# First projection of a two-layer attention kernel in a written order: half of its channels transposed first, its six norms by two powers, epsilon as a column of the squares

## The chip, the cores and the metric

The kernel runs as one program on one core of a Trainium2 chip. The metric is the device time of an execution in microseconds, lower is better. The engines are TensorE (PE; its weight loads are PEld), VectorE (DVE), ScalarE (ACT), GpSimd (POOL) and SyncE (SP, which issues most of the DMAs). Each engine works off its own queue in the order in which the built program lists its instructions, and waits on semaphores of the others.

## The reference, cut to what matters

Two layers over 512 latent tokens and 256 context tokens, model width 1024. What the change touches is the first step of layer 0:

```python
mod_x = silu(c) @ w_ada + b_ada            # shift, scale, gate for latent tokens
mod_c = silu(c_ctx) @ w_ada + b_ada        # the same for context tokens
hx = rmsnorm(x, norm_g) * (1 + scale_x) + shift_x
hc = rmsnorm(ctx, norm_g) * (1 + scale_c) + shift_c
px = hx @ w_in                             # a_k, a_v, b_k, b_v, a_q, b_q, a_z, b_z, g_a, g_b
ka = rmsnorm(a_k per head of 64, k_norm_a) # likewise qa, qb, kb
```

`rmsnorm` divides by sqrt(mean(x*x) + 1e-6). Neighbourhood attention, grouped-query attention, gated merging, an output projection and a residual follow, in both layers; layer 1 computes only the latent stream at its end.

## The kernel before, in words

All products are in fp32 split in a high and a low part (`hi`, `lo`), three TensorE passes of 128x512 each: `hi*whi`, `hi*wlo`, `lo*whi` (lines 352 to 356, `mm3`). The low part is made by a subtraction on DVE or GpSimd (`load_w`, line 316; for weights, 327; for activations, 314).

**The opening of layer 0** builds the normalised, modulated input with channels on partitions. There are six token tiles of 128 (four latent, two context) and eight channel tiles k of 128.

- `load_x` (128) issues the six loads of x on SP, mixed with the small inputs, the first weights of the modulation and the first weight tile of the projection.
- silu of the conditioning vectors is made of a tanh (143) and two DVE operations (145, 146), transposed (151) and copied to `scol`; the small parameters are transposed to `gcol`.
- `start_y` (289), once per token tile: ACT squares the tile and sums (294), GpSimd adds epsilon (261) and raises to -0.5 (263, both in `rstd`, 258), DVE scales the tile (296), TensorE transposes its eight channel blocks in two halves of four (300), DVE copies the first half and ACT the second out of PSUM into `yT` (302).
- The modulation's shift and scale come in five parts, `PARTS` (35): channel tiles 0; 1 and 2; 3 and 4; 5 and 6; 7. A part is `ada_load` (177, one 1 MB load per channel tile), `ada_part` (190: matmuls of four 32-column groups, then a copy of the row on ACT, 199) and `ada_turn` (202: transposes, a reduce, and three small DVE operations in `mod_finish`, 168).
- `start_mod` (304) applies scale and shift to a channel tile in place (311, DVE), casts its high part (313, ACT) and subtracts for the low part (314, DVE, and GpSimd for k = 2 and 5). The first two channel tiles (`START`, 36) go in three pieces of 256 tokens, the others whole.
- The first projection (a_k, lines 594 to 610) holds all six token tiles in six PSUM banks and adds the channel tiles part by part. After the third and the fourth token tile (`AT`, 34) the next part's matmuls and its transposes are put on TensorE.

What orders this: the framework's scheduler, from a simulated timeline, sets the order of each engine's instructions; `behind` (388) pins single groups on one engine behind what was recorded before them.

**After it** the six a_k tiles are copied out of PSUM, squared, reduced and normalised one by one (`evac_na`, 447; `head_rstd`, 409; `mul_heads`, 416), and turned to channels by `turn` (424) some tiles later. `head_rstd` makes a square of 512 columns on ACT (411), a reduce per head on DVE (413) and, through `rstd`, an add and a power on GpSimd. It serves a_k, a_q, b_k and b_q in both layers: 44 calls, 32 of them with 8 heads, 12 with 2. The same `rstd` serves six token tiles in front of layer 1 (`make_hx`, 266). The next projection, a_v, follows at once (line 629): its weights go through three `raw` buffers and are split on ACT, DVE and GpSimd.

Of the kernel before, what the change touches and what calls it, by code (L numbers as in the profile page):

```python
# [14 lines left out]
DM = 1024  # L15
# [17 lines left out]
ON_PE, ON_DVE = mybir.EngineType.PE, mybir.EngineType.DVE  # L33
AT = (2, 3)
PARTS = ((0, 1), (1, 3), (3, 5), (5, 7), (7, 8))
START = 2
# [15 lines left out]
def hybrid_kernel(es: ExitStack, tc, x, ctx, cvec, w_ada, w_ada0, small, gvec, w_in, w_o_a, w_o_b, w_out,  # L52
# [72 lines left out]
    xts0 = []  # L125
    npool = es_n.enter_context(tc.tile_pool(name="nrm", bufs=2, reuse_waits="tile"))

    def load_x(t):
        xt = npool.tile([128, DM], F32, tag="x", name=nm("x"), bufs=XB)
        nc.sync.dma_start(xt, x_src(t))  # L130
        xts0.append(xt)

    load_x(0)
    S.dma_start(ident, ident_d)
    S.dma_start(stg, small)
    nc.sync.dma_start(crow, cvec)
    load_x(1)
    ehalf = cp.tile([128, 8], F32, name="ehalf")
    G.memset(ehalf, -0.5)


    cth = stp.tile([16, 128], F32, name="cth")
    S.activation(cth, crow, AF.Tanh, scale=0.5)
    csl = stp.tile([16, 128], F32, name="csl")
    V.scalar_tensor_tensor(csl, cth, 1.0, crow, ALU.add, ALU.mult)
    V.tensor_scalar(csl, csl, 0.5, None, ALU.mult)
    asum = cp.tile([128, 24, 2, 2], F32, name="asum")
    scol = stp.tile([128, 8, 32], F32, name="scol")
    V.memset(scol, 0.0)
    pt = psw(16, "t")  # L150
    T.transpose(pt, csl, ident[0:16, 0:16])
    V.tensor_copy(scol[:, :, 0:2], pt.rearrange("p (v k) -> p k v", v=2))
    gcol = cp.tile([128, 68], F32, name="gcol")
    pt = psw(68, "t")
    T.transpose(pt, stg, ident[0:68, 0:68])
    V.tensor_copy(gcol, pt)
    bsc = cp.tile([128, 2, 8], F32, name="bsc")
    V.tensor_scalar(bsc, gcol[:, 0:32].rearrange("p (l a k) -> p l a k", l=2, a=2)[:, :, 1, :], 1.0, None, ALU.add)
    g32 = cp.tile([128, 2, 8], F32, name="g32")
    V.tensor_scalar(g32, gcol[:, 32:48].rearrange("p (l k) -> p l k", l=2), 32.0, None, ALU.mult)  # L160
# [3 lines left out]

    def raw_tile():
        return wp.tile([128, 512], F32, tag="raw", name=nm("raw"), bufs=3)
# [10 lines left out]
    def ada_load(q, pool):  # L177

        ws, (k0, k1) = [], PARTS[q]
        for k in range(k0, k1):  # L180
            w = (pool.tile([128, 2048], F32, tag="rawx", name=nm("rawx"), bufs=RX) if k % 2 == 0
                 else big("rawy")[:, 0:2048])
            nc.sync.dma_start(w, w_ada0[k])
            w = w.rearrange("p (i n) -> p i n", n=256 * (k1 - k0))
            ws += [w[:, i, :] for i in range(w.shape[1])]
        return ws

    ada_row = []

    def ada_part(q, ws, pool):  # L190

        k0, k1 = PARTS[q]
        m = k1 - k0
        pt = psw(256 * m, "t")
        for i, w in enumerate(ws):
            j = i % 4
            T.matmul(pt[32 * j:32 * j + 32], scol[:, i, :], w, start=i < 4, stop=i > 3)
        row = pool.tile([128, 512], F32, tag="row", name=nm("row"), bufs=1)
        S.copy(row[:, :256 * m], pt)
        return row  # L200

    def ada_turn(q, row, pool):

        k0, k1 = PARTS[q]
        m = k1 - k0
        pt = psw(256 * m, "t")
        for f in range(2 * m):
            T.transpose(pt[:, 128 * f:128 * f + 128], row[:, 128 * f:128 * f + 128], ident)
        sums = pool.tile([128, 2, 2, 2], F32, tag="sums", name=nm("sums"))
        V.tensor_reduce(sums.rearrange("p a f v -> p (a f) v") if m == 2 else sums[:, :, 0],  # L210
                        pt.rearrange("p (f j v) -> p f v j", f=2 * m, j=4)[:, :, 0:2, :], AX, ALU.add)
        mod_finish(0, sums[:, :, 0:m], k0, k1)
# [45 lines left out]
    def rstd(ss, n, eps_n, w):  # L258

        a = sp.tile([128, 8], F32, tag="rsa", name=nm("rsa"))  # L260
        G.tensor_scalar(a[:, :w], ss, eps_n, None, ALU.add)
        b = sp.tile([128, 8], F32, tag="rsb", name=nm("rsb"))
        G.tensor_tensor(b[:, :w], a[:, :w], ehalf[:, :w], ALU.pow)
        return b[:, :w]

    def make_hx(l, t, xt, hx, pool):
# [4 lines left out]
        rs = rstd(ss, 1, DM * EPS, 1)  # L271
        y = pool.tile([128, DM], F32, tag="y", name=nm("y"), bufs=1)
        V.tensor_scalar(y, xt, rs, None, ALU.mult)
# [15 lines left out]
    def start_y(t, pool, yT):  # L289

        xt = xts0[t]
        junk = pool.tile([128, DM], F32, tag="junk", name=nm("junk"), bufs=1)
        ss = sp.tile([128, 1], F32, tag="ss1", name=nm("ss1"))
        S.activation(junk, xt, AF.Square, accum_out=ss)
        rs = rstd(ss, 1, DM * EPS, 1)
        V.tensor_scalar(xt, xt, rs, None, ALU.mult)
        for h in range(2):
            pt = psw(512, "t")
            for k in range(4):
                T.transpose(pt[:, 128 * k:128 * k + 128], xt[:, 512 * h + 128 * k:512 * h + 128 * k + 128], ident)  # L300
            d = yT[h].rearrange("p (k n) -> p k n", k=4)[:, :, 128 * t:128 * t + 128]
            (S.copy if h else V.tensor_copy)(d, pt.rearrange("p (k n) -> p k n", k=4))

    def start_mod(k, yT, hx, cuts):

        d = yT[k // 4].rearrange("p (k n) -> p k n", k=4)[:, k % 4, :]
        hi, lo = hx_k(hx, 0, k), hx_k(hx, 1, k)
# [180 lines left out]
    def layer(l, hx, nxt, mid):  # L488
# [105 lines left out]
        if first:  # L594
            w, pss = [], [psw() for t in range(6)]
            for q, (k0, k1) in enumerate(PARTS):
                mid(q, lambda: w.extend(load_w(W, C_AK, 512, k1 - k0, mix_lo, k0)))
                for k in range(k0, k1):
                    start_mods(k)
# [569 lines left out]
```

## Time and profile before

| | us |
|---|---|
| median of 3 runs | 1156.32 |
| range of the runs | 1155.41 to 1157.58 |
| the profiled execution's own time | 1156.21 |
| its span, first to last instruction | 1154.4 |
| TensorE busy | 1125.2 (97%) |
| VectorE busy | 811.8 (70%) |
| ScalarE busy | 574.2 (50%) |
| GpSimd busy | 496.5 (43%) |

Durations come from the profiled execution. Matmuls are pipelined: the time of one in the timeline contains its latency, and the distance between two starts is its slot. A row of the timeline is: start, time, engine, line, operation, output and inputs, shape, count, and in brackets how long the engine was idle before and what ended it. A row of the groups is: line, engine, operation, tiles, count, then busy time, mean ns of one, then the idle time before them and its releaser.

### The profile page before, as it was taken

How to read it: one execution, taken by the hardware profiler on the slowest of the kernel's cores; microseconds unless marked ns; L12 is line 12 of the kernel's file. 1: busy time of each engine (PE TensorE's matmuls, PEld its weight loads, DVE VectorE, ACT ScalarE, POOL GpSimd, SP SyncE). 2: the span in 40 equal slices, each digit the busy share in tenths (PEclk: the TensorE clock that was granted, in tenths of full speed). 3: DMA queues.
4: the chain of work that ended last, by engine and by line, in shares of the span. 5: the costliest groups of instructions: out<-in, count | busy, mean ns of one | idle time of the engine just before them, and what ended most of it. 6: DMA issues, size and time to landing. Idle time of an engine off the chain costs nothing.

```text
span 1154.4 us, 17322 instructions
## 1 busy us (share of the span) xinstructions
PE 1125.2 (97%) x6094; PEld 947.6 (82%) x6094; DVE 811.8 (70%) x1512; ACT 574.2 (50%) x1168; POOL 496.5 (43%) x459
## 2 busy tenths in 40 slices
PE   6999999999999999999999999999999999999998
PEld 4688888989988888878788787888888988887786
DVE  5566588997464687698488755569787665798563
ACT  5353266666333465566330265346666445766521
POOL 2362354454265243354411127245563664365321
PEclk9999999999999999999999999999999999999999
DMA  9534222233332332370343423543332333142233
GB/s 380 186 122 138 71 83 65 83 113 97 107 128 65 105 101 73 72 271 19 131 161 103 171 74 110 179 106 113 104 105 82 110 101 102 64 173 92 64 127 93
DMA packets 87999, 134.04 MB, mean 116 GB/s; under 512 B 10628, under 2 KB 52584, under 8 KB 86248
## 3 DMA queue, kind: packets, MB, share of 16 engines
q1 hardware_dynamic: 87696, 132.83, 35.6%
q8 instruction: 48, 0.79, 0.3%
q14 instruction: 39, 0.32, 0.1%
q10 hardware_dynamic: 216, 0.10, 0.0%
HBM read 115.58 MB, written 17.32 MB: 115 GB/s over the span
## 4 chain that ended last, share of the span: by engine, by line
PE 80%; DVE 9%; issue 4%; ACT 3%; POOL 2%; DMA 2%; SPq 0%; POOLq 0%; ACTq 0%; DVEq 0%
PE psx L356 11%; PE psx L354 11%; PE psx L355 11%; PE psf L354 9%; PE psf L356 9%; PE psf L355 9%; PE pst L676 4%; PE pss L725 2%; PE pss L726 2%; PE psv L980 2%; PE pss L802 1%; PE psv L979 1%; PE pst L429 1%; DVE ptl L680 1%; DVE wlo L341 1%
## 5 line engine op out<-in xcount | busy, mean ns | idle before, releaser
L680 DVE TENSOR_TENSOR ptl<-pst,pth 128x512 fp32r<-128x512 f32 (+1 forms) x176 | 116.0, 671 | 46.6 <-ACT pth L679 45.6
L679 ACT CAST pth<-pst 128x512 fp32r<-128x512 f32 (+1 forms) x176 | 99.3, 576 | 87.1 <-PE pst L676 56.1
L341 POOL TENSOR_TENSOR wlo<-raw,whi 128x512 fp32r<-128x512 f32 x68 | 95.6, 1411 | 104.8 <-ACT whi L339 84.1
L354 PE MATMUL psf<-hx,whi 128*128 128x512 f32 (+1 forms) x368 | 139.2, 378 | 1.0 <-ACT zt L514 1.0
L355 PE MATMUL psf<-hx,whi 128*128 128x512 f32 (+1 forms) x368 | 138.2, 375 | 0.0
L356 PE MATMUL psf<-hx,wlo 128*128 128x512 f32 (+1 forms) x368 | 137.9, 375 | 0.0
L354 PE MATMUL psx<-whi,hx 128*128 128x512 f32 (+1 forms) x368 | 137.8, 376 | 0.0
L355 PE MATMUL psx<-wlo,hx 128*128 128x512 f32 (+1 forms) x368 | 135.6, 368 | 0.0
L356 PE MATMUL psx<-whi,hx 128*128 128x512 f32 (+1 forms) x368 | 134.9, 369 | 0.0
L327 POOL TENSOR_TENSOR wlo<-raw,whi 128x512 fp32r<-128x512 f32 x44 | 63.6, 1447 | 137.6 <-ACT whi L324 121.0
L339 ACT CAST whi<-raw 128x512 fp32r<-128x512 f32 x136 | 82.5, 621 | 55.0 <-DMA raw<-in_w_in_dram 36.5
L324 ACT CAST whi<-raw 128x512 fp32r<-128x512 f32 x96 | 58.6, 622 | 101.2 <-PE psx L356 39.9
L676 PE MATMUL pst<-ident,p 128*128 128x128 f32 x640 | 99.9, 272 | 1.4 <-DVE ptl L680 0.8
L341 DVE TENSOR_TENSOR wlo<-raw,whi 128x512 fp32r<-128x512 f32 x68 | 71.5, 1053 | 29.7 <-ACT whi L339 29.0
L676 PEld LDWEIGHTS pst<-ident,p 128*128 128x128 f32 x640 | 77.8, 140 | 13.0 <-DVE ptl L680 1.3
L665 POOL TENSOR_SCALAR r<-r 128x1 f32<-128x1 f32 x64 | 22.5, 351 | 152.5 <-DVE r L660 145.5
L666 POOL TENSOR_TENSOR p<-p,r 128x512 f32<-128x512 f32 (+1 forms) x64 | 84.2, 1315 | 5.1 <-POOL r L665 0.2
L354 PEld LDWEIGHTS psx<-whi,hx 128*128 128x128 f32 x368 | 69.5, 189 | 13.5 <-issue 2.9
L356 PEld LDWEIGHTS psf<-hx,wlo 128*128 128x128 f32 x368 | 69.4, 189 | 11.8
L354 PEld LDWEIGHTS psf<-hx,whi 128*128 128x128 f32 x368 | 69.4, 189 | 11.8 <-ACT zt L514 1.2
L356 PEld LDWEIGHTS psx<-whi,hx 128*128 128x128 f32 x368 | 69.4, 189 | 11.7
L355 PEld LDWEIGHTS psx<-wlo,hx 128*128 128x128 f32 x368 | 69.6, 189 | 10.6
(239 smaller groups left out, 3033.8 us busy)
## 6 DMA issues: line engine op xcount, KB each, us to landing
raw<-in_w_in_dram SPq DMA_DIRECT2D x168, 256.0 KB, 2.9
rawb<-in_w_ada_dram SPq DMA_DIRECT2D x64, 256.0 KB, 2.7
gs<-zt SPq DMA_DIRECT2D x32, 256.0 KB, 2.0
raw<-in_w_out_dram SPq DMA_DIRECT2D x32, 256.0 KB, 2.9
tg<-gs SPq DMA_DIRECT2D x4, 1536.0 KB, 6.7
rawx<-in_w_ada_dram SPq DMA_DIRECT2D x4, 1024.0 KB, 9.1
rawy<-in_w_ada_dram SPq DMA_DIRECT2D x4, 1024.0 KB, 8.9
raw<-in_w_o_a_dram SPq DMA_DIRECT2D x16, 256.0 KB, 2.8
```

What stands on the lines that cost most here:

```text
L324: S.copy(hi[:, :n], raw[:, :n])
L327: e.tensor_tensor(lo[:, :n], raw[:, :n], F(hi[:, :n]), ALU.subtract)
L339: S.copy(hi, raw)
L341: lo_eng(i).tensor_tensor(lo, raw, F(hi), ALU.subtract)
L354: T.matmul(ps, lhs[0], rhs[0], start=first, stop=False)
L355: T.matmul(ps, lhs[0], rhs[1], start=False, stop=False)
L356: T.matmul(ps, lhs[1], rhs[0], start=False, stop=last)
L666: G.tensor_tensor(p[:, c0:c1], p[:, c0:c1], r[:, i:i + 1].to_broadcast([128, c1 - c0]), ALU.mult)
L676: T.transpose(pt[:, c0:c0 + 128], src, ident)
L679: S.copy(hi[:, n0:n1], pt[:, n0:n1])
L680: V.tensor_tensor(lo[:, n0:n1], pt[:, n0:n1], F(hi[:, n0:n1]), ALU.subtract)
L725: T.matmul(ps[:, c0:c0 + n], q, sl(kh), start=True, stop=False)
```

## The change

It does three things.

1. **The opening and the first projection are written out by hand** (`start`), and `in_turn` pins the written order on TensorE, DVE, ACT and GpSimd. `wake` puts matmuls of a zero tile on TensorE at three places (six, one and three of 128x256). Only the first four channel blocks of each token tile are transposed ahead of the first products (`start_turn(t, 0)`); the second halves (`start_turn(t, 1)`) follow during k = 0, 1 and 2. The modulation goes in the parts 0; 1; 2 and 3; 4 and 5; 6 and 7, and every channel tile in three pieces of 256 tokens. All low parts of this stage are on DVE. The products run channel tile by channel tile.
2. **Epsilon rides along.** The token tiles get a 1025th column that holds sqrt(1024 * 1e-6), the heads' squares a 65th that holds 64 * 1e-6, so that the sum contains it, and the add on GpSimd goes, except in `make_hx`.
3. **The six norms of a_k** are summed in two groups of three tiles (24 columns each), with one power for each group.

The core of the diff:

```diff
-PARTS = ((0, 1), (1, 3), (3, 5), (5, 7), (7, 8))
-START = 2
+PARTS = ((0, 1), (1, 2), (2, 4), (4, 6), (6, 8))
+TURN = (1, 3)
+AKG, YB = ((0, 1, 2), (3, 4, 5)), 5
+WT = (0, 1)
...
     def load_x(t):
-        xt = npool.tile([128, DM], F32, tag="x", name=nm("x"), bufs=XB)
-        nc.sync.dma_start(xt, x_src(t))
-        xts0.append(xt)
+        xe = npool.tile([128, DM + 1], F32, tag="x", name=nm("x"), bufs=XB)
+        G.memset(xe[:, DM:DM + 1], (DM * EPS) ** 0.5)
+        xe0.append(xe)
+        xts0.append(xe[:, 0:DM])
+        nc.sync.dma_start(xts0[t], x_src(t))
...
+    ada_load(0)
+    load_raw(0)
+    for t in range(2, 6):
+        load_x(t)
+    for k in (1, 2):
+        ada_load(k)
+        load_raw(k)
+    ada_load(3)
...
+    V.memset(zero, 0.0)
+    S.activation(cth, zero[0:16, 0:128], AF.Tanh)
...
+    def wake(n, cols):
+        pt = psw(512, "t")
+        for i in range(n):
+            T.matmul(pt[:, :cols], zero[:, 0:128], zero[:, :cols], start=True, stop=True)
...
+    def start_ss(t):
+        junk = npool.tile([128, DM + 1], F32, tag="junk", name=nm("junk"), bufs=1)
+        ss = sp.tile([128, 1], F32, tag="ss1", name=nm("ss1"))
+        S.activation(junk, xe0[t], AF.Square, accum_out=ss)
+
+        def rest():
+            G.tensor_tensor(ss, ss, ehalf[:, 0:1], ALU.pow)
+            V.tensor_scalar(xts0[t], xts0[t], ss, None, ALU.mult)
+        return rest
...
+    def head_ss(ps, nh, ss):
+        sq = hp["sq"][0]
+        hp["sq"].reverse()
+        S.activation(sq[:, :nh, 0:HD], ps.rearrange("p (h d) -> p h d", d=HD), AF.Square)
+        V.tensor_reduce(ss, sq[:, :nh], AX, ALU.add)
+
+    def head_pow(ss, n):
+        G.tensor_tensor(ss, ss, ehalf[:, :n], ALU.pow)
...
+            def evac_ak(ts):
+                n = 8 * len(ts)
+                ss = sp.tile([128, 32], F32, tag="ss32", name=nm("ss32"), bufs=1)
+                for i, t in enumerate(ts):
+                    y = hp["p"].tile([128, 512], F32, tag="y", name=nm("y"), bufs=YB)
+                    (V.tensor_copy if t % 2 else S.copy)(y, pss[t])
+                    head_ss(y, 8, ss[:, 8 * i:8 * i + 8])
+                    ys.append(y)
+                head_pow(ss[:, :n], n)
+                for i, t in enumerate(ts):
+                    mul_heads(ys[t], ys[t], ss[:, 8 * i:8 * i + 8], 8)
+                    to_channels(ys[t], 4, kav, t, False, gk)
...
+    def in_turn(fn):
+        for e in (ON_PE, ON_DVE, ON_ACT, ON_POOL):
+            fn = lambda e=e, fn=fn: behind(e, fn)
+        fn()
...
+        def body():
+            wake(6, 256)
+            norm0 = start_ss(0)
+            tanh()
+            norm0()
+            silu()
+            norm1 = start_ss(1)
+            silu_b()
+            constants()
+            out0 = start_turn(0, 0)
+            wake(1, 256)
+            row0 = ada_part(0)
+            out0(S.copy)
+            norm1()
+            out1 = start_turn(1, 0)
+            hi0 = split_hi(raw0[0])
+            w.append(split_lo(raw0[0], hi0, V))
+            row0()
+            mod0 = ada_turn(0)
+            wake(3, 256)
+            out1(V.tensor_copy)
+            norm2 = start_ss(2)
+            mod0()
+            lo = start_mod(0, 0, 256)
+            norm3 = start_ss(3)
+            norm2()
+            prod(0, 0, 0)
+            prod(0, 1, 0)
+            lo(V)
...
+            for k in range(1, KT):
+                q = next(i for i, (k0, k1) in enumerate(PARTS) if k0 <= k < k1)
+                more = k == PARTS[q][0] and q + 1 < len(PARTS)
+                pieces = [(256 * i, 256 * i + 256) for i in range(3)]
+                for t in range(6):
+                    prod(k, t)
+                    if more and t == TURN[0]:
+                        row = ada_part(q + 1)
+                        row()
+                    if more and t == TURN[1]:
+                        ada_turn(q + 1)()
+                    if k + 1 < KT:
+                        d = t - (3 if k == 1 else 0)
+                        if 0 <= d < 3:
+                            los.append(start_mod(k + 1, *pieces.pop(0)))
+                            if d > 0:
+                                los.pop(0)(V)
+                        if d == 2:
+                            los.pop(0)(V)
+                        if t == WT[0]:
+                            hi = split_hi(raw0[k + 1])
+                        if t == WT[1]:
+                            w.append(split_lo(raw0[k + 1], hi, V))
+                    if later and t % (4 - k) == 0:
+                        start_turn(later.pop(0), 1)(S.copy)
+                    if t == 4 and k + 3 < KT:
+                        load_raw(k + 3)
+                        if k + 4 < KT:
+                            ada_load(k + 4)
...
```

In the built program SP issues, after the first nine loads, the modulation weights and weight tiles as their buffers come free; the two broadcast loads of `cd` (the silu vectors) and the first two tiles of layer 1's modulation (`rawb`) stand ahead of the second weight tile of a_v, where before they stood behind all eight. Beside this stage the instructions of the rest of the program are the same but for the norms' adds and tiles, in an order that the scheduler has changed at some places.

288 lines of the change are left out of this document (162 added, 126 removed).

## The prediction

> **What bounds the kernel now.** I read the page first, then the windows (columns: length, TensorE, its weight loads, VectorE, ScalarE, GpSimd, granted clock, DMA share, GB/s), the waits and the timeline of the first 70 us.
>
> ```profile
> PE 1125.2 (97%) x6094; PEld 947.6 (82%) x6094; DVE 811.8 (70%) x1512; ACT 574.2 (50%) x1168; POOL 496.5 (43%) x459
> ```
> ```profile
> 0.00:10.00 10.00, 2.56 (x10) 1.93 (x10) 3.44 (x12) 4.05 (x7) 1.93 (x9) 1.00 0.84 297
> 10.00:20.00 10.00, 8.08 (x54) 5.68 (x55) 6.34 (x16) 8.20 (x17) 4.56 (x9) 1.00 1.02 420
> 60.00:70.00 10.00, 10.00 (x46) 8.17 (x45) 7.26 (x12) 7.90 (x15) 5.77 (x6) 1.00 0.34 103
> ```
> ```profile
> PE pst L151 <- DVE csl L146: 6.6, 1, 6.6
> PE pst L429 <- ACT sq L411: 0.7, 1, 0.7
> ```
>
> TensorE is busy for 97% of the span and idle for 29.2 us; 9.4 of these lie in the first 20 us (the second and the first window: 10 - 2.56 and 10 - 8.08). From 60 us on its windows are full. So time can be won in the opening, until the first product and through the first projection, and a microsecond won there goes through to the end. The head norms hardly hold TensorE: one wait of 0.7 us is charged to a chain with a norm in it.
>
> The timeline gives the stage's marks.
>
> ```profile
> 7.72 1.97 PE L300 MATMUL pst<-ident,x 128*128 128x128 f32 x8 [0.51 <-DVE scol L152]
> ...
> 11.97 1.94 PE L197 MATMUL pst<-rawx,scol 128*32 128x256 f32 x16
> ...
> 14.68 1.09 PE L300 MATMUL pst<-ident,x 128*128 128x128 f32 x8
> ...
> 18.20 1.09 PE L300 MATMUL pst<-ident,x 128*128 128x128 f32 x8 [0.68 <-DVE yT L302]
> ...
> 19.05 0.47 PE L354 MATMUL psf<-whi,hx 128*128 128x512 f32 x1
> ...
> 20.53 0.60 PE L300 MATMUL pst<-ident,x 128*128 128x128 f32 x4
> ...
> 20.89 0.48 PE L354 MATMUL psx<-whi,hx 128*128 128x512 f32 x1
> ...
> 27.42 0.50 PE L354 MATMUL psf<-whi,hx 128*128 128x512 f32 x1 [0.31 <-ACT hx L313]
> ```
> ```profile
> 32.10 1.07 PE L197 MATMUL pst<-rawy,scol 128*32 128x512 f32 x8
> ...
> 33.96 0.50 PE L354 MATMUL psx<-whi,hx 128*128 128x512 f32 x1
> ...
> 55.58 1.07 PE L197 MATMUL pst<-rawy,scol 128*32 128x256 f32 x16
> 56.58 0.50 PE L354 MATMUL psx<-whi,hx 128*128 128x512 f32 x1
> ...
> 65.16 0.39 PE L354 MATMUL psf<-whi,hx 128*128 128x512 f32 x1
> ```
> ```profile
> 19.53 0.23 PE psf L355
> ```
>
> The first product starts at 19.05, the second channel tile (k = 1) at 27.42, the next projection at 65.16. A product's slot is 0.23 us (the chain). A modulation part of two tiles takes 1.86 (32.10 to 33.96), of one tile 1.00 (55.58 to 56.58) where TensorE is quick, and four transposes 0.36 (20.53 to 20.89). TensorE also has a slow state: eight transposes took 1.97 at 7.72 and 1.09 at 14.68, one tile's part 1.94 at 11.97 and 1.00 later, though the granted clock stands at 1.00 in all these windows. So between 27.42 and 65.16 there are 37.7 us, of which 126 products are 29.0, three parts 1.86 + 1.86 + 1.00 = 4.7, three small turns at most 1.1: some 2.9 us were waits.
>
> **The change part by part.** The sum is against the profiled run's own 1156.21 us (span 1154.4 and 1.8 around it), 0.1 below the median of 1156.32. The terms are these rows (the groups of 0 to 64 us with shapes apart; then loads).
>
> ```profile
> L296 DVE TENSOR_SCALAR x<-x,rsb 128x1024 f32<-128x1024 f32 x6 | 4.5, 752 | 2.2 <-POOL rsb L263 2.2
> L302 DVE COPY yT<-pst 128x512 f32<-128x512 f32 x6 | 4.1, 685 | 1.6 <-PE pst L300 1.6
> L302 ACT COPY yT<-pst 128x512 f32<-128x512 f32 x6 | 3.5, 586 | 5.3 <-PE pst L300 5.2
> L263 POOL TENSOR_TENSOR rsb<-rsa,ehalf 128x1 f32<-128x1 f32 x6 | 3.5, 575 | 0.5
> L314 DVE TENSOR_TENSOR hx<-yT,hx 128x256 fp32r<-128x256 f32 x6 | 2.4, 422 | 0.7 <-ACT hx L313 0.7
> L313 ACT CAST hx<-yT 128x256 fp32r<-128x256 f32 x6 | 2.3, 408 | 2.0 <-DVE yT L311 2.0
> L311 DVE TENSOR_SCALAR yT<-yT,modc 128x256 f32<-128x256 f32 x12 | 4.7, 409 | 0.1
> L199 ACT COPY row<-pst 128x256 f32<-128x256 f32 x2 | 0.7, 372 | 5.4 <-PE pst L197 5.4
> L324 ACT CAST whi<-raw 128x512 fp32r<-128x512 f32 x15 | 8.8, 619 | 1.4 <-DMA raw<-in_w_in_dram 1.4
> ```
> ```profile
> 6.50 1.16 ACT junk L294 x2
> ```
> ```profile
> 23.51 0.69 DVE L327 TENSOR_TENSOR wlo<-raw,whi 128x512 fp32r<-128x512 f32 x1
> ...
> 25.83 0.18 DVE L210 TENSOR_REDUCE sums<-pst 128x8 f32<-128x32 f32 x1
> ...
> 26.52 1.84 DVE L311 TENSOR_SCALAR yT<-yT,modc 128x256 f32<-128x256 f32 x5
> ```
> ```profile
> 2.10 0.43 SPq L183 DMA_DIRECT2D rawx<-in_w_ada_dram  x1
> ...
> 5.31 1.11 SPq L130 DMA_DIRECT2D x<-in_ctx_dram  x2
> ```
> ```profile
> DMA to landing us min/median/max: 6.9/9.1/12.7
> ```
> ```profile
> x<-in_ctx_dram SPq DMA_DIRECT2D x1, 512.0 KB, 8.7
> ```
>
> *Opening.* The first nine loads keep their order on SP, so the first modulation weights land at 9.0 (2.10 + 6.9) and the last token tile near 14.7 (the second of the pair, issued near 6.0, + 8.7). All else that the first part needs (x0 scaled, silu turned) is small work that I put done by 8.7. The part therefore starts at 9.1 instead of 11.97, because x1's and half of x0's transposes no longer stand ahead of it, and takes 1.0 instead of 1.94 if the six zero matmuls, issued from about 1.2 us, have made TensorE quick: done at 10.1. Row copy 0.37 and two transposes: 10.9. DVE must first do x1's scaling, a weight's low part and x1's copy (0.69) and is free at 11.6; reduce and three small operations are 0.69 (25.83 to 26.52): 12.3. Scale-and-shift 0.41, cast 0.41, some 0.05 a hand-off: **first product at 13.3**, 5.8 earlier. The zero matmuls themselves lie where TensorE waits; only the single one ahead of the first part can cost, at most 0.2.
>
> *Rest of k = 0.* On ACT the squares of x3, x4, x5 now stand behind that cast: 3 x 1.16 from 13.2 to 16.7 (x5 is there in time), then x3's copy to 17.3; DVE, after x4's scaling, ends the second piece's scale-and-shift at 17.8; cast 18.2: third and fourth token tile. TensorE's six products end at 19.7, x5's transposes 20.1, second part 21.1; ACT copies x5 (20.2 to 20.8), splits a weight 0.62, and after DVE's scale-and-shift casts the third piece at 22.0; k = 0 ends at 23.5. The second part's sums reach DVE at 22.9; 0.69 + 0.41 + 0.41 with hand-offs: **k = 1 starts at 24.5**, 2.9 ahead of now. Of 5.8 half is given back: TensorE waits about 3 us of these 11 for ACT and DVE.
>
> *k = 1 to 7.* More work has been put off than now: five second-half transposes 5 x 0.36 = 1.8, and the parts left are 3 x 1.86 = 5.6. With 29.0 of products and three turns 1.1 this is 37.5 us: 62.0 without any wait. Waits that the order leaves: 0.2 for a PSUM bank in k = 1, and 0.1 where k = 2 begins (its chain from the turn is 0.69 + 0.41 + 0.41 and hand-offs, 1.75, against 0.36 + 6 x 0.23 of cover). From then on each piece is made a channel tile ahead: DVE has 3 x 0.41 + 3 x 0.42 + 0.7 (a weight's low part, 23.51) = 3.2 us a tile against 4.1 of products, now that GpSimd makes no low parts here. I take 0.3 of waits, between 0 and the 2.9 of now: next projection at 62.3 instead of 65.16, **-2.9**.
>
> *The order of loads.* From k = 1 on each weight tile waits on SP for the split three tiles before, with a modulation load behind it. The fifth of these (for k = 2's part at 33.7) is issued near 22.7, the seventh near 35 for 45; the longest landing above, 12.7, would cost 1.7 and 2.7, the median nothing. I take nothing.
>
> *Norms.*
>
> ```profile
> L263 POOL TENSOR_TENSOR rsb<-rsa,ehalf x56: 569/1666/2149, 6.2 to 934.9; 128x8 f32<-128x8 f32 x32, 128x1 f32<-128x1 f32 x12, 128x2 f32<-128x2 f32 x12
> L261 POOL TENSOR_SCALAR rsa<-ss x56: 218/244/743, 5.9 to 934.6; 128x8 f32<-128x8 f32 x32, 128x1 f32<-128x1 f32 x12, 128x2 f32<-128x2 f32 x12
> ```
>
> 50 of the 56 adds go (the six in front of layer 1 stay): 50 x 0.24 = 12 us of GpSimd, which is busy 43%. Six powers of 8 columns, 6 x 1.67 = 10.0, become two of 24. No row shows 24 columns: from 0.575 for one and 1.67 for eight, 0.16 a column, I estimate 4.2 each; three times the longest row, 6.4, is the other end, three times 0.57 the low one. The first can begin when the third square is summed, near 67, and its tile's transposes stand some 56 slots behind the new projection's start, near 75: 67 + 4.2 + 0.7 = 72 or, at 6.4, 74. Hidden. Reduces over 65 columns instead of 64, eight small memsets and 1025 columns in a square are under 2% of their rows, beside TensorE. Waits of TensorE on norms: 0.7 and little else; I take **-0.4**, between 0 and -1.0.
>
> Sum: 1156.21 - 2.9 - 0.4 = 1152.9; on the median's footing **1153.0 us**.
>
> [...] The rows show that 16 transposes from 7.72 did not make TensorE quick and that it was quick at 14.68, 2.7 us after ordinary matmuls began at 11.97. [...]
>
> **The rivals.**
> - *TensorE is slow where I count it quick* (zeros do not warm it, or it falls back between the products of k = 0). For: 7.72. Against: 18.20. Price: the part +0.94 and x0's and x1's half transposes +0.4 each ahead of the first product, or about 2.7 us of doubled work after 18.3, so 1.4 to 2.7: 1155.2.
> - *The fixed order keeps the waits*: four engines each in one written order, so that every piece waits for the last of DVE and ACT; 2.9 of waits stay, or k = 1 starts nearer 27. 1156.0. For: half the lead is lost in k = 0 already. Against: 3.2 of DVE against 4.1.
> - *Slower: the next projection's weights come late.* They go through three buffers, and SP now issues the two broadcast loads and two modulation tiles ahead of the second of them. The fourth waits for GpSimd's low part of the first, near 56.8, and is needed at 64.3 after 1.3 of splitting; 6.0 us of landing decide.
>
> ```profile
> DMA to landing us min/median/max: 2.5/3.4/11.3
> ```
>  At the longest, 11.3, TensorE would stand 5.3: 1158.3. Against: the DMA share is 0.34 at 60 us, and 3.4 is the middle.
> - *That it does not do what it says* is out: the built program's instructions stand in the new order on all four engines, and the rest differs little.
>
> **How the numbers follow.** Forecast 0.58 (1151.5 to 1154.6), slow TensorE 0.15, waits kept 0.17, late weights 0.10. A measurement of this kernel tells about 0.2%, 2.3 us, from no change: faster means below 1154.0. Of the forecast 0.5 lies below, 0.08 above; of the two middle rivals 0.02 below, 0.28 within, 0.02 above; late weights are 0.02 within (a small delay) and 0.08 above. Faster 0.52, same 0.38, slower 0.10. The range leaves a tenth on each side: 1150.8 (no waits, norms -1.0, a walk 0.9 shorter) to 1157.4 (the lower late-weights cases).
>
> **What would show it.** First product at 13.3 and not past 14.5; the first part at 1.0 us; k = 1 at 24.5; the next projection at 62.3, after gaps that sum to 0.3; two powers of about 4 us with no wait at the transposes near 75; the rest at its present length. It is wrong if TensorE's 128-column transposes still take 0.25 us after 8 us, if k = 1 begins after 26, or if the new projection waits for whi or wlo.

## The result, and the profile of the changed kernel

The changed kernel took 1151.69 us (median of 8 runs, 1150.48 to 1154.22) where the kernel before took 1155.47 (8 runs, 1153.94 to 1157.58): ratio 0.9969, 95% interval 0.9959 to 0.9978, so 3.8 us less. A second comparison of the same two kernels (11 runs and 33) gave 0.9977, 0.9968 to 0.9986, 2.7 us less. The forecast was 1153.0. The sum came out near; two of its terms did not, and one of the rivals takes part in most executions, as far as their mean granted clock tells.

The profiled run of the changed kernel took 1150.48 us (span 1148.7), the fastest of its eight, and that of before 1156.21, slower than its median. The two profiles therefore stand 5.7 us apart where the medians stand 2.7 to 3.8: one profile must not be read as the kernel here.

Totals of the changed kernel's page, then its first windows (columns: length, TensorE, its weight loads, VectorE, ScalarE, GpSimd, granted clock, DMA share, GB/s):

```profile
PE 1127.1 (98%) x6114; PEld 951.2 (83%) x6114; DVE 811.4 (71%) x1541; ACT 578.8 (50%) x1185; POOL 467.1 (41%) x405
```
```profile
0.00:10.00 10.00, 7.44 (x28) 5.12 (x32) 3.13 (x12) 4.94 (x9) 1.63 (x13) 1.00 0.83 294
10.00:20.00 10.00, 8.09 (x51) 5.40 (x43) 6.80 (x15) 7.00 (x14) 2.37 (x4) 1.00 1.02 414
```

TensorE's idle time in the first 10 us fell from 7.4 to 2.6, most of it filled with zeros; what the opening gained has to be read from marks. The timeline of TensorE, in the places that the prediction named:

```profile
1.17 5.49 PE L187 MATMUL pst<-zero 128*128 128x256 f32 x12 [1.17 <-DVE zero L179]
...
9.58 1.07 PE L231 MATMUL pst<-rawx,scol 128*32 128x256 f32 x16
...
13.53 0.50 PE L1141 MATMUL psf<-whi,hx 128*128 128x512 f32 x1
...
24.60 0.53 PE L1141 MATMUL psf<-whi,hx 128*128 128x512 f32 x1 [0.25 <-ACT hx L350]
...
25.44 0.60 PE L338 MATMUL pst<-ident,x 128*128 128x128 f32 x4
25.79 0.48 PE L1141 MATMUL psx<-whi,hx 128*128 128x512 f32 x1
26.11 0.39 PE L1142 MATMUL psx<-wlo,hx 128*128 128x512 f32 x1
...
63.35 0.39 PE L401 MATMUL psf<-whi,hx 128*128 128x512 f32 x1
```

First product 13.53 (forecast 13.3), second channel tile 24.60 (24.5), next projection 63.35 (62.3; 65.16 before). So in this execution the opening is worth 1.8 us and not 2.9. The rows from 25.44 show one reason: four transposes take 0.35 until the product behind them starts, and that product takes 0.32 where the others take 0.23. The other 3.9 us of the two spans' difference lie behind the first projection, and need another account.

The waits of TensorE hold the first hint of it. The row of before in which a norm held TensorE (0.7 us, near 704) has no successor; the largest rows that are left are those of before, the one of L199 apart, which was 6.6 there (L151):

```profile
PE psv L1042 <- DVE ptl L742: 2.0, 3, 1.5
PE pst L736 <- DVE ptl L742: 1.5, 3, 0.8
PE pst L199 <- DVE csl L195: 1.3, 1, 1.3
PE psx L401 <- DVE ho L751: 1.2, 1, 1.2
```

### The profile page after: what moved, and what is told of

Its sections match the earlier page's. It is cut to its first block, busy times and chain, and to the rows that moved or that the text cites. A ratio compares the mean times of both kernels' runs of the same rounds, so it can differ in the third digit from the quotient of the medians.

```text
span 1148.7 us, 17395 instructions
## 1 busy us (share of the span) xinstructions
PE 1127.1 (98%) x6114; PEld 951.2 (83%) x6114; DVE 811.4 (71%) x1541; ACT 578.8 (50%) x1185; POOL 467.1 (41%) x405
## 4 chain that ended last, share of the span: by engine, by line
PE 84%; DVE 6%; ACT 3%; DMA 2%; issue 2%; POOL 1%; SPq 0%; ACTq 0%; POOLq 0%; DVEq 0%
PE psx L403 12%; PE psx L402 12%; PE psx L401 12%; PE psf L401 9%; PE psf L402 9%; PE psf L403 9%; PE pst L738 5%; PE pss L787 2%; PE pss L788 2%; PE pss L864 2%; PE psv L1042 2%; PE pst L487 1%; PE psv L1041 1%; DMA rawb<-in_w_ada_dram 1%; DVE ptl L742 1%
## 5 line engine op out<-in xcount | busy, mean ns | idle before, releaser
L388 POOL TENSOR_TENSOR wlo<-raw,whi 128x512 fp32r<-128x512 f32 x68 | 96.3, 1419 | 99.1 <-ACT whi L386 76.2
L374 POOL TENSOR_TENSOR wlo<-raw,whi 128x512 fp32r<-128x512 f32 x40 | 55.2, 1381 | 163.1 <-ACT whi L371 155.3
L401 PE MATMUL psx<-whi,hx 128*128 128x512 f32 (+1 forms) x328 | 121.3, 371 | 0.0
L402 PE MATMUL psx<-wlo,hx 128*128 128x512 f32 (+1 forms) x328 | 119.9, 366 | 0.0
L403 PE MATMUL psx<-whi,hx 128*128 128x512 f32 (+1 forms) x328 | 119.9, 365 | 0.0
L386 ACT CAST whi<-raw 128x512 fp32r<-128x512 f32 x136 | 82.7, 622 | 55.2 <-DMA raw<-in_w_in_dram 39.7
L371 ACT CAST whi<-raw 128x512 fp32r<-128x512 f32 x88 | 54.0, 622 | 103.1 <-PE psx L403 37.0
L466 POOL TENSOR_TENSOR ss<-ss,ehalf 128x8 f32<-128x8 f32 (+2 forms) x40 | 63.5, 1589 | 49.8 <-DVE ss L463 48.4
L401 PEld LDWEIGHTS psf<-hx,whi 128*128 128x128 f32 x368 | 69.4, 189 | 11.0 <-ACT zt L576 0.4
L402 PEld LDWEIGHTS psf<-hx,whi 128*128 128x128 f32 x368 | 69.5, 189 | 10.4
L725 DVE TENSOR_SCALAR p<-p,r 128x512 f32<-128x512 f32 (+2 forms) x96 | 72.5, 769 | 2.4
```

Of the source, the lines that this page charges most:

```text
L374: e.tensor_tensor(lo[:, :n], raw[:, :n], F(hi[:, :n]), ALU.subtract)
L386: S.copy(hi, raw)
L388: lo_eng(i).tensor_tensor(lo, raw, F(hi), ALU.subtract)
L401: T.matmul(ps, lhs[0], rhs[0], start=first, stop=False)
L402: T.matmul(ps, lhs[0], rhs[1], start=False, stop=False)
L403: T.matmul(ps, lhs[1], rhs[0], start=False, stop=last)
```

## The experiments

Twelve kernels, in three groups of four; those of a group ran on one chip with the kernel before among them (31, 33 and 14 runs of it, medians 1155.01, 1155.33 and 1155.05). The last column is read from their profiles (us); in the kernel before it is 65.16.

| kernel | median us | ratio to before (95%) | next projection starts |
|---|---|---|---|
| norms_only | 1153.19 | 0.9983 (0.9974, 0.9992) | 65.10 |
| opening_only | 1154.21 | 0.9993 (0.9984, 1.0002) | 64.77 |
| six_powers | 1153.60 | 0.9992 (0.9982, 1.0002) | 64.92 |
| adds_back | 1152.96 | 0.9980 (0.9971, 0.9990) | 63.32 |
| no_zeros | 1154.01 | 0.9991 (0.9982, 1.0000) | 65.89 |
| both_halves | 1153.49 | 0.9985 (0.9976, 0.9993) | 65.37 |
| free_order | 1156.51 | 1.0010 (1.0002, 1.0019) | 68.48 |
| after_again | 1152.64 | 0.9977 (0.9968, 0.9986) | 66.19 |
| kept_warm | 1149.96 | 0.9951 (0.9939, 0.9964) | 63.30 |
| eight_zeros | 1149.84 | 0.9950 (0.9938, 0.9963) | 64.45 |
| warm_opening_only | 1152.34 | 0.9975 (0.9966, 0.9985) | 63.49 |
| before_zeros | 1160.84 | 1.0042 (1.0029, 1.0055) | 68.47 |

### The two halves of the change apart

**norms_only** is the kernel before with the changed treatment of the heads:

```diff
-        S.activation(sq[:, :64 * nh], ps, AF.Square)
-        V.tensor_reduce(ss[:, :nh], sq[:, :64 * nh].rearrange("p (h d) -> p h d", d=64), AX, ALU.add)
-        return rstd(ss[:, :nh], nh, HD * EPS, nh)
+        head_ss(ps, nh, ss[:, :nh])
+        head_pow(ss[:, :nh], nh)
+        return ss[:, :nh]
...
-            for t in range(5):
-                ev(t, pss[t])
+            evac_ak(AKG[0])
```

> The kernel before, with its own opening, and of the change only the norms of the heads: epsilon as a 65th column of the squares, no add, two powers of 24 columns for the first projection. Theory A (the sizes of the prediction: norms 0.4 us): 1155.1 where the kernel before has 1155.5, ratio 0.9997, TensorE's next projection at 65.2 as before. Theory B (the two traces: the two kernels stand 1.8 us apart at 63 us and 5.7 at the end, so that most of the gain is made behind the opening, by the norms): 2 us or more, 1153.5 or less, ratio at most 0.998, and the waits of the kernel before at 704 us (0.7, for a norm's square), at 321 (0.3) and at 957 (1.0) gone. Theory C (the later part of the gain is no effect of the norms but of where the shorter opening puts the loads): ratio 1.000, the three waits stay.

**opening_only** is the reverse: the changed kernel's opening, the heads' norms of before.

> The changed kernel with the norms of the heads as before (64 columns, an add and a power for each tile, six powers in the first projection); the opening in its explicit order stays. Theory A: 2.9 us of opening, 1152.6, ratio 0.9975. Theory B: 1.8 us of opening and nothing behind it, 1153.7, ratio 0.9984, the waits at 704, 321 and 957 us back, next projection at 63.3. Theory C: the whole gain, 1151.7, ratio 0.997, without those waits.

Measured: the norms alone 1.8 us, the opening alone 0.8. Both results contradict theory A: the norms are not 0.4 us, and the opening on its own is hardly to be told from nothing. Theory C fails too, since the norms without the new opening do gain. Of theory B's three waits only one is the norms'. That of 0.3 near 321 us and that of 1.0 near 957 us are gone in opening_only too, which has the old norms (and 0.5 of the latter is left in norms_only): they come and go between kernels. That near 704 is back in opening_only, and gone in norms_only.

### Which part of the norms

**six_powers** keeps the epsilon column and gives each tile of the first projection its own power:

```diff
-            evac_ak(AKG[0])
+            for t in range(5):
+                ev(t, pss[t])
```

> The changed kernel with a power for each tile in the first projection (six of 8 columns, five tiles ahead of the next projection's products and one behind the first, as before), epsilon still a column. If the norms gain by the two powers of 24 columns: 1 to 2 us longer than the changed kernel, ratio to the kernel before 0.998 to 0.9985. If they gain by the adds that are gone (the chain of every later norm is 0.25 us and a hand-off shorter): as the changed kernel, 0.997. Theory A: no difference, 0.997.

**adds_back** keeps the two powers and puts the add back:

```diff
+        G.tensor_scalar(ss, ss, HD * EPS, None, ALU.add)
         G.tensor_tensor(ss, ss, ehalf[:, :n], ALU.pow)
```

> The changed kernel with the add of epsilon on GpSimd ahead of each power and squares of 64 columns again; the two powers of 24 columns stay. If the norms gain by the adds that are gone: 1 to 2 us longer than the changed kernel, ratio to the kernel before 0.998 to 0.9985, with the waits at 704, 321 and 957 us back. If by the two powers: as the changed kernel, 0.997. Theory A: 0.3 us longer at most, 0.9972.

The medians do not tell the two apart (0.9992 and 0.9980, intervals that overlap; their own runs spread over 6.2 and 3.5 us, see below): adds_back came out where a gain by the adds had put it, but six_powers is slower than both of its expectations. So the traces have to. In the first projection the grouping gains nothing: from the start of the next projection to 150 us (the first scores) opening_only, with six adds and six powers, takes 86.61 us, and the changed kernel 86.61 too. (six_powers itself takes 87.10, but the 0.5 more builds up from 99 to 136 us, behind its last power, which ends at 82.6.) One place where something is gained is layer 1. From the last value product of layer 0 (561 us in the changed kernel) to the first value product of layer 1 (798) the five kernels with an add (before, opening_only, warm_opening_only, adds_back, before_zeros) take 238.3 to 241.4 us, the nine without one 236.2 to 238.1. The chain there, with the add (warm_opening_only, of the group below, ScalarE, GpSimd, VectorE and TensorE):

```profile
697.52 1.08 ACT L462 ACTIVATE sq<-psx 128x512 f32<-128x512 f32 x2
...
699.08 0.25 POOL L455 TENSOR_SCALAR rsa<-ss 128x8 f32<-128x8 f32 x1
...
699.42 2.15 POOL L457 TENSOR_TENSOR rsb<-rsa,ehalf 128x8 f32<-128x8 f32 x1
...
701.60 0.69 DVE L468 TENSOR_TENSOR y<-psx,rsb 128x512 f32<-128x512 f32 x1
...
702.43 0.63 PE L480 MATMUL pst<-ident,y 128*128 128x128 f32 x4 [0.71 <-ACT sq L462]
```

and without it (kept_warm):

```profile
696.84 1.08 ACT L462 ACTIVATE sq<-psx 128x512 f32<-128x512 f32 x2
...
698.27 3.27 POOL L466 TENSOR_TENSOR ss<-ss,ehalf 128x8 f32<-128x8 f32 x2
...
700.09 0.68 DVE L475 TENSOR_TENSOR y<-psx,ss 128x512 f32<-128x512 f32 x1
...
700.92 0.63 PE L487 MATMUL pst<-ident,y 128*128 128x128 f32 x4
```

From the squares to the transposes it is 4.9 us with the add and 4.1 without, and the transposes stand only two tiles behind: with the add TensorE waits 0.7, without it not at all. The releaser that the row names (the squares) had long been done; the late one is the scaled tile `y`. This wait of 0.7 stands in all five kernels with an add and in none of the nine without (of the three waits that were expected back in adds_back, it alone came); so does a wait of 0.2 to 0.5 for the first scores' maximum near 797 us. Together that is 0.9 to 1.2 us where there is an add.

This does not settle the norms' 1.8 us. norms_only lacks these two waits, but has one of 1.1 for a tile `za` at 782 us instead, so its waits from 561 to 801 us sum to 3.8 us, as those of before do to 3.7. And of the 2.9 us between the profiles of these two kernels only 0.9 arise in that stretch; 1.0 stand before it and 1.1 behind it.

A second part of the difference lies in the products themselves. Where two products follow each other without a wait, behind 70 us (some 2900 pairs in each profile), the mean distance of their starts is 229.1 ns in before and 228.6 in norms_only, which over all pairs is 1.5 us. In opening_only, warm_opening_only and before_zeros it is 228.9, 229.0 and 229.1, in the changed kernel and its other variants 228.6, but in six_powers 229.2 and in adds_back 228.3. So it doesn't go with the adds, and what sets it is open. It also blurs the two experiments above: against the first profile of the changed kernel it costs six_powers 1.7 us and gives adds_back 0.9, as much as they were to show. That the adds cost the two waits is seen in the rows; that they are the norms' 1.8 us is not shown.

The powers of 24 columns, in the changed kernel:

```profile
66.91 4.69 POOL L466 TENSOR_TENSOR ss<-ss,ehalf 128x24 f32<-128x24 f32 x1
...
82.19 4.49 POOL L466 TENSOR_TENSOR ss<-ss,ehalf 128x24 f32<-128x24 f32 x1 [1.18 <-DMA raw<-in_w_in_dram]
```

4.7 and 4.5 us where 4.2 was estimated, and hidden: TensorE has no wait at the transposes from 76.06 on.

### What the opening hangs on

**no_zeros** takes the three groups of zero matmuls out:

```diff
-            wake(6, 256)
...
-            wake(1, 256)
...
-            wake(3, 256)
```

> The changed kernel without the ten matmuls over zeros. If they are what makes TensorE quick in the opening: the eight transposes and the first part take double (0.25 a transpose, 1.94 for the part at about 9.5 us), the first product stands near 15.2 instead of 13.5, and of these 1.7 us 1.0 to 1.7 reach the end: 1152.7 to 1153.4, ratio to the kernel before 0.9976 to 0.9982. If TensorE becomes quick without them, or is not bound there: the part 1.07, ratio 0.997. If the quick state is also lost between the products of the first channel tile without them (the rival of the prediction): up to 2.7 us, 1154.4.

**after_again** is the changed kernel unchanged.

> The changed kernel once more, for a second profile and for its time on the chip of the three others: ratio 0.9969 with an interval of some 0.001, next projection near 63.35 us, and the waits at 704, 321 and 957 us again absent if their absence belongs to the kernel and not to one execution; with the first profile's span of 1148.7 within 2 us.

no_zeros is 1.4 us slower than after_again in the same group (1154.01 and 1152.64). Its transposes take 1.12 us for four instead of 0.66 and its first part 1.94 instead of 1.07, as expected, and its first product stands at 14.95:

```profile
8.65 1.12 PE L338 MATMUL pst<-ident,x 128*128 128x128 f32 x4
9.70 1.94 PE L231 MATMUL pst<-rawx,scol 128*32 128x256 f32 x16
...
14.95 0.50 PE L1141 MATMUL psf<-whi,hx 128*128 128x512 f32 x1 [1.84 <-ACT hx L350]
```

Its median lies between the first expectation (to 1153.4) and the last (1154.4), and the last one's loss between the products of the first channel tile is there too, from 20.4 to 23.8 us (below).

More is learned from after_again's profile. It is the same program as the first profile, and its opening is 2.8 us longer: next projection 66.19 instead of 63.35, later than before the change. Its windows of 6 us, the seventh number being the granted clock:

```profile
0.00:6.00 6.00, 4.33 (x12) 3.26 (x12) 0.54 (x2) 2.94 (x5) 0.54 (x12) 1.00 0.73 234
6.00:12.00 6.00, 4.14 (x24) 2.20 (x24) 3.29 (x11) 2.25 (x4) 1.09 (x2) 0.63 1.00 402
12.00:18.00 6.00, 5.64 (x19) 4.24 (x16) 3.29 (x9) 4.14 (x9) 1.16 (x3) 0.51 1.04 423
18.00:24.00 6.00, 5.07 (x40) 3.65 (x40) 2.81 (x6) 3.10 (x7) 1.04 (x2) 1.00 1.02 416
```
and its TensorE rows:
```profile
1.17 4.33 PE L187 MATMUL pst<-zero 128*128 128x256 f32 x12 [1.17 <-DVE zero L179]
7.80 0.28 PE L199 MATMUL pst<-ident,csl 16*128 16x16 f32 x1 [2.30 <-DVE csl L195]
...
10.38 1.94 PE L231 MATMUL pst<-rawx,scol 128*32 128x256 f32 x16
...
16.51 0.99 PE L1141 MATMUL psf<-whi,hx 128*128 128x512 f32 x1
```

The zeros did make TensorE quick, and earlier than in the first profile (4.33 us for the same twelve rows instead of 5.49). Then it stood idle from 5.50 to 7.80, the clock fell to half at 7.6, and the part took 1.94 instead of 1.07. The loads are no cause of it: the first modulation weights landed at 8.84 us here and at 9.04 in the first profile. Narrower windows show how long a fall lasts. In opening_only:

```profile
7.00:8.00 1.00, 0.12 (x1) 0.12 (x1) 0.79 (x3) 0.00 (x0) 0.00 (x0) 1.00 0.96 350
8.00:9.00 1.00, 0.94 (x5) 0.77 (x6) 0.65 (x4) 0.93 (x1) 0.00 (x0) 0.60 0.93 330
...
11.00:12.00 1.00, 1.00 (x16) 0.44 (x8) 0.13 (x1) 0.62 (x1) 0.00 (x0) 0.70 1.03 422
12.00:13.00 1.00, 1.00 (x10) 0.62 (x6) 0.79 (x2) 0.75 (x2) 0.00 (x0) 1.00 1.00 410
```

A mean of 0.60 between 1.00 and 0.50 puts the fall at 8.2, one of 0.70 the rise at 11.6: 3.4 us. Read in the same way it lasted 3.4 in six_powers (8.5 to 11.9), both_halves (9.6 to 13.0), free_order (8.7 to 12.1) and no_zeros (20.4 to 23.8), and 10.2, three times 3.4, in after_again (7.6 to 17.8). The first profile and adds_back have none. One fall of 3.4 us at the first part moves the first product from 13.60 (adds_back) to 15.16 (six_powers). (In opening_only the first weights also landed 1.4 us later than in most others, at 10.48, for which its part waited 0.3 us.) So each of these falls lasted 3.4 us or three times that, and those in front of the first product began anywhere from 7.6 to 9.6 us after the start.

Which execution falls is to be told, without a profile, only by the mean granted clock of a run: of the 19 runs of the changed kernel five have 0.999 (1150.5 to 1151.0 us), seven 0.998 (1151.7 to 1152.6) and seven less (1152.4 to 1155.3). The inference is not strict: where the last microseconds of a profile were read, they also are at half clock, from 0.2 us (before) to 3.2 us (opening_only), which by itself takes up to 0.0014 off the mean, so that the seven at 0.998 are falls by their times and not by a trace. The eleven of norms_only, with the old opening, have 0.999 or 1.000 and lie within 1.6 us.

### The order and the half turn

**both_halves** turns all channels of a token tile where the changed kernel turns the first half; **free_order** lets the scheduler place the opening's instructions:

```diff
-        in_turn(body)
+        body()
```

> The changed kernel with all channels of a token tile turned where it turned the first half (both groups of four transposes, one copy on ScalarE and one on VectorE), so that none is left for the later channel tiles. TensorE has the same transposes. If the half turn is what lets the first channel tile start early: six more copies of 0.57 to 0.69 us, 1.9 on each of ScalarE and VectorE ahead of the second channel tile, of which 1 to 2 us reach it (second channel tile near 26, then 2.2 us less to turn): the end 0 to 0.5 us later, ratio 0.997 to 0.9975. If the later transposes are free because they lie beside other work: the end 1.5 to 2 us later, ratio 0.9985.

> The changed kernel with the same instructions in the opening, but not held in the written order on TensorE, VectorE, ScalarE and GpSimd: the scheduler puts them. If the written order is what takes the waits out of the first projection: 1 to 3 us longer than the changed kernel, ratio 0.998 to 0.9995, with the waits of TensorE from 24 to 63 us back. If the work that is put off and the earlier first part are enough: 0.997.

both_halves: 0.8 us more than after_again in the same group, between the two expectations when it is set against that kernel, and with a fall of its clock in the profile, so it decides little. Against six_powers, whose fall was as long, its first product stands 1.3 us later (16.42 and 15.16) and its second channel tile 2.2 (28.45 and 26.22), as the extra copies would have it, and its next projection 0.5 later (65.37 and 64.92). free_order is plain: 3.9 us more than after_again, and slower than the kernel before. TensorE's waits in it between 23 and 64 us:

```profile
PE psf L1141 <- ACT hx L350: 2.2, 1, 2.2
PE pst L246 <- ACT row L235: 0.8, 1, 0.8
PE pst L338 <- DVE sums L250: 0.3, 1, 0.3
```

3.3 us, where after_again has 0.8 in the same stretch. Behind the longest of them the clock falls a second time, from 59.9 to 63.3 us, where the products stand 0.43 us apart instead of 0.23 (a row of the timeline and one of the windows):

```profile
58.55 0.50 PE L1141 MATMUL psf<-whi,hx 128*128 128x512 f32 x1 [2.19 <-ACT hx L350]
```
```profile
60.00:61.00 1.00, 1.00 (x3) 0.73 (x3) 1.00 (x4) 0.00 (x0) 0.00 (x0) 0.50 1.09 113
```

So the written order takes waits out, and with them a fall; without it the same instructions lose more than the whole gain.

### The clock held

**kept_warm** gives the first group eight zero matmuls, and fills three gaps of the first channel tile with more, written into the accumulator of token tile 5, whose first product overwrites them (a line that takes the six accumulators ahead of the first product is left out here):

```diff
-            wake(6, 256)
+            wake(8, 256)
...
+            fill(256)
             out3 = start_turn(3, 0)
+            fill(256)
...
             out4 = start_turn(4, 0)
+            fill(128)
```

> The changed kernel with eight zero matmuls in place of six at the start, and three more in the gaps of TensorE between the third, fourth and fifth token tile's transposes (into the bank that the sixth token tile's products overwrite later). Theory W (the spread of the changed kernel's runs, 1150.5 to 1155.3, comes from TensorE's clock falling to half where a stretch of some 3.4 us has too little work, 9.8 us long in one profile and absent in another): no window of the first 30 us with a granted clock below 1.00, first product at 13.5, next projection at 63.4, median 1150.8 to 1151.3, ratio 0.9963, all runs within 2 us. Rival R (the spread comes from the landing of loads or from the end of the kernel): the same 4 to 5 us of spread and 0.997 to 0.9975; the added zeros may cost 0.3.

**eight_zeros** has the first of these edits alone, **warm_opening_only** is opening_only with all of them, and **before_zeros** is the kernel before with six zero matmuls at its start.

> The changed kernel with eight zero matmuls in place of six at the start and nothing else. Theory W: the fall near 8 us is gone, the chance of one in the gaps of the first channel tile (near 18 to 20 us) stays; median 1151.0 to 1151.7, ratio 0.9965, single runs up to 1153. Rival R: as the changed kernel, 0.9973, and a start later by up to 0.3.

> The opening of the changed kernel with the zeros of the run above (eight, and three in the gaps), the norms of the heads as before the change. Theory W: the opening alone was worth 0.8 us (ratio 0.9993) because its clock fell in most runs; held quick it gives the 1.9 us between the two first profiles, 1153.2 to 1153.6, ratio 0.9984, and with the 1.8 of the norms the whole gain. Rival R: 0.9990 to 0.9993, as without the added zeros.

> The kernel before with six zero matmuls at the start and nothing else: is the quick clock by itself what the opening gains? If it is: the sixteen first transposes and the first part take half, 2.9 us less of TensorE ahead of the first product, next projection near 63.5, ratio 0.9985. If the first product there waits for the other engines (the copies of four token tiles stand ahead of it): at most 0.7 us, ratio 0.9994 or more.

Theory W holds, and rival R does not: kept_warm takes 1149.96, 5.1 us less than before, its runs lie within 1.2 us (1149.29 to 1150.44), and its windows carry a full clock. In size it came out 0.8 us below the theory's 1150.8 to 1151.3, and below the 1150.87 of the changed kernel's runs at 0.999; on a chip where before is 0.3 to 0.4 us quicker, half of that stays without a row to account for it.

```profile
6.00:12.00 6.00, 5.08 (x36) 2.98 (x34) 3.98 (x13) 3.66 (x7) 1.15 (x2) 1.00 1.00 401
12.00:18.00 6.00, 5.72 (x30) 4.24 (x30) 4.52 (x12) 4.70 (x11) 2.27 (x4) 1.00 1.03 420
18.00:24.00 6.00, 5.28 (x39) 3.60 (x39) 3.19 (x10) 2.54 (x6) 0.00 (x0) 1.00 1.03 416
```

eight_zeros is as quick at the median; its profiled run (1150.66, its slowest) shows the late fall that the three fills guard against, from 18.9 to 22.4, and a next projection at 64.45:

```profile
12.00:18.00 6.00, 4.84 (x24) 3.33 (x24) 4.52 (x12) 4.58 (x11) 2.38 (x4) 1.00 1.04 424
18.00:24.00 6.00, 5.47 (x31) 3.51 (x32) 2.28 (x5) 2.55 (x6) 0.00 (x0) 0.72 1.02 414
```

Runs up to 1153, as theory W had them for this kernel, did not occur. Whether the fills are worth anything at the median is not shown. warm_opening_only: the opening alone is now worth 2.7 us (0.9975) instead of 0.8, more than the expected 1.9; its next projection stands at 63.49, 1.7 us ahead of before. The remaining 1.0 isn't located: before's profile has a wait of 1.0 near 957 us that this one lacks, but how many runs of the kernel before have it isn't known.

before_zeros refutes both of its expectations: 5.8 us slower. The zeros make it quick near 4.9 us (an estimate from their twelve rows, 4.67 us long where the first profile of the changed kernel has 5.49), it falls at 8.3 and stays at half until 21.9, 13.6 us or four times 3.4, through the transposes and the part:

```profile
6.00:12.00 6.00, 3.64 (x17) 3.10 (x18) 3.41 (x12) 2.65 (x7) 2.45 (x5) 0.69 1.02 415
12.00:18.00 6.00, 4.46 (x28) 2.42 (x27) 2.65 (x8) 4.61 (x9) 3.05 (x7) 0.50 1.02 426
18.00:24.00 6.00, 5.80 (x27) 4.75 (x26) 4.14 (x8) 2.79 (x6) 1.40 (x3) 0.67 1.03 419
```

At 150 us its profile stands 3.3 behind that of before. Another 2.6 arise from the last value product of layer 0 to the first of layer 1, where TensorE waits 1.4 at 778 us for a scaled tile `y` of a norm, as it does not in before; why was not followed up. Zeros at the start are no gain by themselves: here, behind 3.4 us that TensorE's rows cover to 0.46, the clock fell, and the next projection stands at 68.47 where without zeros it stands at 65.16.

## Why the prediction was right, point by point

It forecast 3.3 us and 2.7 to 3.8 were measured, but by two errors of opposite sign: the opening alone gave 0.8 of its 2.9, the norms alone 1.8 for 0.4. That the total came out so near is luck.

- *Opening: right where the clock holds.* First part 9.58 and 1.07 us (forecast 9.1 and 1.0; the single zero matmul ahead of it held TensorE for 0.66, from 8.92, where at most 0.2 was allowed), first product 13.53 (13.3), second piece 18.35 (18.2), second part 20.40 (20.1), k = 1 at 24.60 (24.5). In the execution that was profiled first the walk holds to 0.3 us at every product.
- *k = 1 to 7: mis-sized by 0.9 us.* "37.5 us work + waits 0.3" came out as 38.75, with waits of 0.2. The missing term is the price of a switch: the first product behind a group of transposes takes 0.09 more than the others (25.79 to 26.11), and there are eleven such groups (three parts, three turns, five second halves). The same shape stands in the rows of before that the prediction quoted (20.53, then 20.89 at 0.48), and I priced the transposes alone. For the same reason the "2.9 us were waits" of the kernel before was too much: its trace has 1.3 us of waits there (0.8, 0.3 and 0.2). So 1.8 us at 63 us, not 2.9.
- *Rival "TensorE is slow where I count it quick": not excluded, but true of most executions.* I gave it 0.15 as one of several cases of which one would hold. Whether the clock falls differs between executions of one program: by their mean clock 14 of 19 runs have a fall, and it puts the median 1.4 us higher (1152.23 for all 19, 1150.87 for the five at 0.999). My argument against it, the row at 18.20 of before (eight transposes in 1.09, behind nothing but transposes from 13.91 on), was about a stretch in which TensorE was mostly busy (idle for 0.68 us at most); the fall, in six of the eight profiles that have one, comes within or at most 1.7 us behind the idle stretch of 1.2 to 2.3 us between the zeros' end and the silu's transpose, which the prediction took for time "where TensorE waits" and so for free. The 2.7 us that it put on a fall after 18.3 no run shows: that of eight_zeros, from 18.9 to 22.4, goes with a next projection at 64.45, 1.15 behind that of kept_warm.
- *Rival "the fixed order keeps the waits": refuted.* free_order shows the waits return when the order is taken away.
- *Rival "late weights": refuted.* No profile has a wait at the start of the next projection, at 63 to 69 us. Its price for the worst landing, 1158.3, also lay below the 1158.6 or so from which a result would have counted as slower, so the 0.08 that it was given there had no price behind it.
- *Norms: mis-sized, 0.4 for 1.8.* The wait of 0.7 near 704 us was seen, quoted, and priced below its size; it went entirely. "From 60 us on its windows are full" was read from one window: 18.5 of TensorE's 29.2 us of idle time lie behind 60 us. That in layer 1 the norms' chain stands on the path (4.9 us from squares to transposes, two tiles of cover) was missed, and so was the distance of the products (229.1 ns to 228.6, some 1.5 us), whose cause is still open. Two powers instead of six: nothing, as forecast, and 4.7 us each against 4.2.

## What to carry to other kernels

Where TensorE is woken by filler work, the filler should last until the real work starts, and thin stretches behind it are a risk: in after_again 2.3 us of idleness behind the zeros went with a clock at half from 7.6 to 17.8 us. Woken too early and then left idle it can be worse than not woken, as in before_zeros, 5.8 us slower than the kernel before. A profile of one execution can't show this (the next projection of one program stood at 63.35 us in the first profile and at 66.19 in the second): profile the same program twice, and look at the granted clock in windows of 1 us and at the spread of the runs before the median. And a serial chain through a slow engine (here squares, sum, add, power, scaling) is priced at each place where its consumer stands close behind, not by the total of the waits that carry its name. Where variants differ by a microsecond or two, look at the mean distance of the products too: from 228.3 to 229.2 ns between kernels with the same products, which over some 2900 pairs is 2.6 us.

## What the runs showed of the hardware

- The clock fell without a long idle stretch. In the eight profiles with a fall, TensorE's rows (transposes among them) cover 0.35 to 0.57 of the 3.4 us ahead of it. The longest single idle stretch ahead of the fall was 2.3 us in after_again, and 0.6 us in eight_zeros. The share alone does not decide: from 15.5 to 18.9 us it is 0.57 in eight_zeros and in the first profile of the changed kernel, and only in eight_zeros the clock fell.
- The granted clock read 1.00 before its first change even where TensorE was slow: in the first profile of the changed kernel the first twelve zero rows took 5.49 us (0.46 each) at 1.00, six of them at 12.02 took 1.56 (0.26 each), also at 1.00. In these traces the durations, not the column, told the clock until the first fall.
- A power on GpSimd took much the same per column, grouped or not: 24 columns took 4.5 to 4.7 us, 0.19 to 0.20 each, two powers of 8 side by side in kept_warm 3.27 and one of 8 in six_powers, its shortest, 1.64, 0.20 to 0.21 each. Against the sum of these (4.91) grouping saved 0.2 to 0.4 us for 24.
- The slot of a product was not constant: at full clock and without a wait, starts of neighbouring 128x512 products stood mostly 0.22 to 0.24 us apart (in before 0.23 in 1956 pairs, 0.22 in 581, 0.24 in 319), and the mean behind 70 us went from 228.3 (adds_back) to 229.2 (six_powers) between kernels with the same products.
